# A Mamba-2 scan block's share of the carried state: per-head products against a decayed C, or one 512-column product scaled by token and added by identity products

## The chip, the core and the metric

One core of a Trainium2 chip runs the whole program. The metric is device time in microseconds: 2370.83 us is the median of three timed runs (2366.95 to 2382.75). Five engines work side by side, each through its own instructions in order: TensorE (PE, matrix products; PEld its weight loads), VectorE (DVE), ScalarE (ACT), GpSimd (POOL) and SyncE (SP, which issues DMAs). The tensor engine's clock has two levels in the records, 2.4 GHz (a granted clock of 1.00) and 1.2 GHz (0.50).

## The reference, cut to what matters

The model is two layers deep; layer 0 has a Mamba-2 mixer, layer 1 attention, both between feed-forward blocks. A prompt of 512 tokens and a running stream of 32 tokens (with its old state) go through together. The mixer has 32 heads of 64 channels in 4 groups of 8, and a state of 128 numbers for each channel. The scan that the change touches:

```python
def step(state, inp):
    x_c, a_c, B_c, C_c = inp
    a_cs = jnp.cumsum(a_c, axis=1)
    seg = a_cs[:, :, None] - a_cs[:, None, :]
    decay = jnp.exp(jnp.where(causal, seg, -jnp.inf))
    cb = jnp.einsum('bign,bjgn->bijg', C_c, B_c)
    y_diag = jnp.einsum('bijg,bijge,bjgep->bigep', cb, decay, x_c)
    y_off = jnp.einsum('bign,bgepn->bigep', C_c, state) * jnp.exp(a_cs)[..., None]
    w_end = jnp.exp(a_cs[:, -1:] - a_cs)
    new_state = state * jnp.exp(a_cs[:, -1])[..., None, None] + jnp.einsum(
        'bjgn,bjge,bjgep->bgepn', B_c, w_end, x_c)
    return new_state, y_diag + y_off
```

`y_off` is the share of the carried state in a block's outputs: C times the state, times a decay that depends on token and head alone.

## The kernel before

The kernel takes 128 tokens to a block: four blocks c = 0 to 3 of the prompt and a tail, c = 4, with the 32 tokens of the running stream. Channels lie on partitions and tokens in the free dimension, so `y` is [channels, tokens].

All dense products, written to the PSUM tile `mm`, split each float32 matrix into a high and a low part (`whi`, `wlo`) and make three products per chunk, each in two halves of 272 columns. In the Mamba layer the dense units run in the order of `MSEQ`, "i0 z0 i1 i2 z1 o0 i3 z2 o1 z3 o2 o3": inputs (B, C and four x units), gates and output products of the four groups. Each input unit goes through a short convolution (`cu`, `cv` on DVE and ACT) before the scan reads it. The buffers of B, C and x (`grp`) exist twice, so the inputs of group 2 start when the scan of group 0 is complete.

The order of all instructions is made at build time by `Plan`: every piece of work is a generator that asks for an engine ("T", "V", "W" for DVE reading PSUM, "S", "G") with an estimated cost, for a slot of a buffer ("get", "put") or for an event ("wait", "set"). `Plan.run` always takes the request that can start first, ranked by the chains' order, and what it emits is kept in that program order on each engine. Dense products have the last rank and fill what the scan leaves free. The estimated costs set the order only.

For each group g and block c the function `ssd` starts these chains: `turn_x` (four PE transposes of x, then `xd` = x times dt on DVE, `xw` on POOL), `turn_b` (transpose of B, `btok`), `decay` (the product of C and B, masked to `cb` on DVE; the decay factors `ex` by eight ACT instructions, an exponential, and DVE's product with `cb`), `state` (one 512-column product `xw,btok`, and the new state `st` by POOL and DVE), and `output`. The tile `ab` holds the running sums of a for all 8 heads, copied to all 128 partitions by a DMA from `acs_d` (`load_ab`).

The share of the carried state goes like this before: `decay_ab` (line 1176 on) exponentiates `ab` in place on ACT, copies its last column to `fade` on DVE, and for c > 0 multiplies it by C on POOL, giving eight decayed copies of C, [128, 8 x n]. `output` then adds to each head's product `ex,xd` a second product `ab,st` (the head's state as weights, its decayed C as moving data) in the same PSUM region. A head has 64 channels, so two heads fill the 128 output partitions, one in each column half of the array.

Of the kernel before, what the change touches and what calls it, by code (L numbers as in the profile page):

```python
# [4 lines left out]
F32 = mybir.dt.float32  # L5
# [5 lines left out]
P = 128  # L11
# [167 lines left out]
def _body(tc, io):  # L179
# [22 lines left out]
    with ExitStack() as ctx:  # L202
# [734 lines left out]
        def mamba(norm, after, ready, ahead):  # L937
            with tc.tile_pool(name="mt", bufs=1, reuse_waits="tile") as tmp, \
# [6 lines left out]
                def aux():  # L945
                    return pa.tile([P, 512], F32, tag="aux", name="aux")

                plan = Plan({"mm": 2, "aux": 4, "raw": 2, "w": 2, "cu": 2, "cv": 2, "grp": 2, "z": NZB, "y": NY, "yh": NYH,
                             "ab": 2, "ex": 2, "xd": 2, "xw": 2, "cb": 1, "btok": 1, "st": 3, "fade": 2}, "m")
                chunks = [(c * P, P) for c in range(NCH)] + [(TP, TS)]  # L950
                tok = tmp.tile([P, 5, 96], F32, tag="tok", name="tok")
                cstate = tmp.tile([P, 24, 6], F32, tag="cstate", name="cstate")
# [7 lines left out]
                def steps(ps):  # L960

                    cost = v_cost(T)
                    yield "wait", "r"
                    rv = halves(norm.r[:, :])
                    v = hm("dv", "ex", 2)
                    yield "W", cost, lambda: V.tensor_tensor(out=halves(v[:, :]), in0=ps[0:32, :, :H], in1=rv[0:32], op=ALU.mult)
                    yield "put", "mm"
                    yield "S", 0.15, lambda: S.activation(acoef, alog, AF.Exp), "exp"
                    yield "V", 0.08, lambda: V.tensor_scalar(acoef, acoef, -1.0, None, op0=ALU.mult)
                    yield "V", cost, lambda: V.tensor_scalar(v, v, dtb, None, op0=ALU.add)  # L970
                    e = hm("de", "ex", 2)
                    yield "V", cost, lambda: V.scalar_tensor_tensor(out=e, in0=v, scalar=-1.0, in1=v, op0=ALU.mult, op1=ALU.min)
                    yield "S", s_cost(T), lambda: S.activation(e, e, AF.Exp), "exp"
                    s = hm("ds", "xd", 2)
                    yield "V", cost, lambda: V.tensor_scalar(s, e, 2.0, None, op0=ALU.add)
                    yield "V", 3.5, lambda: V.reciprocal(s, s)
                    yield "V", cost, lambda: V.tensor_tensor(out=s, in0=s, in1=e, op=ALU.mult)
                    s2 = hm("dw", "xd", 2)
                    yield "V", cost, lambda: V.tensor_tensor(out=s2, in0=s, in1=s, op=ALU.mult)
                    q = hm("dq", "xw", 2)  # L980
                    yield "V", cost, lambda: V.tensor_scalar(q, s2, 1.0 / 17.0, None, op0=ALU.mult)
                    for k in (15, 13, 11, 9, 7, 5, 3):
                        yield "V", cost, lambda: V.scalar_tensor_tensor(out=q, in0=q, scalar=1.0 / k, in1=s2, op0=ALU.add, op1=ALU.mult)
                    yield "V", cost, lambda: V.scalar_tensor_tensor(out=q, in0=q, scalar=1.0, in1=s, op0=ALU.add, op1=ALU.mult)
                    yield "V", cost, lambda: V.tensor_scalar(q, q, 2.0, None, op0=ALU.mult)
                    dtt = hm("dt", "st", 3)
                    yield "V", cost, lambda: V.scalar_tensor_tensor(out=dtt, in0=v, scalar=0.0, in1=q, op0=ALU.max, op1=ALU.add)
                    a = hm("da", "xw", 2)
                    yield "V", cost, lambda: V.tensor_scalar(a, dtt, acoef, None, op0=ALU.mult)
                    keep = hm("keep", "ab", 2)  # L990

                    def starts():
                        G.memset(keep, 1.0)
                        for c in range(5):
                            G.memset(keep[:, c * P:c * P + 1], 0.0)
                    yield "G", 1.0, starts
                    acs = hm("acs", "st", 3)
                    yield "V", 2 * cost, lambda: V.tensor_tensor_scan(acs, keep, a, 0.0, ALU.mult, ALU.add)
                    nc.scalar.dma_start(acs_d, acs)
                    wend = hm("wend", "st", 3)  # L1000

                    def ends():
                        for o, n in chunks:
                            S.activation(wend[:, o:o + n], acs[:, o:o + n], AF.Exp, scale=-1.0, bias=acs[:, o + n - 1:o + n])
                    yield "S", 5 * s_cost(P), ends, "exp"
                    for c, (o, n) in enumerate(chunks):
                        yield "get", "aux"
                        pt = aux()

                        def turn():  # L1010
                            for j, src in enumerate((acs, dtt, wend)):
                                TE.transpose(pt[:n, j * 32:(j + 1) * 32], src[:, o:o + n], ident[:32, :32])
                        yield "T", 0.3, turn
                        yield "W", v_cost(96), lambda: V.tensor_copy(tok[:n, c, :], pt[:n, 0:96])
                        yield "put", "aux"
                    yield "set", "tok"

                def scale():
# [155 lines left out]
                    yield "set", ("ex", g, c)  # L1174

                def decay_ab(g, c, ab):
                    off, n = chunks[c]
                    src = off if c < 4 else SOFF
                    ct = got["C", g][:, src:src + n]
                    yield "S", s_cost(8 * n), lambda: S.activation(ab, ab, AF.Exp), "exp"  # L1180
                    yield "get", "fade"
                    fade = got["fade", g, c] = tmp.tile([P, 8, 1], F32, tag="fade", name="fade", bufs=2)
                    yield "V", 0.08, lambda: V.tensor_copy(fade, ab[:, :, n - 1:n])
                    yield "set", ("fade", g, c)
                    if c > 0:
                        yield "G", 0.06 + 8 * n * 2.28e-3, lambda: G.tensor_tensor(out=ab, in0=ab, in1=ct.unsqueeze(1).to_broadcast([P, 8, n]), op=ALU.mult)
                    yield "set", ("cd", g, c)

                def turn_x(g, c):
                    off, n = chunks[c]  # L1190
# [75 lines left out]
                def output(g, c):  # L1266
                    off, n = chunks[c]
                    src = off if c < 4 else SOFF
                    xs = got["x", g]
                    need = [("ex", g, c), ("xd", g, c), ("xw", g, c), ("cd", g, c)]  # L1270
                    yield "wait", *need
                    if c > 0:
                        yield "wait", ("st", g, before(c))
                    if c == 0:
                        yield "get", "y"
                        got["y", g] = tmp.tile([P, 4, T], F32, tag="y", name="y", bufs=NY)
                        yield "set", ("y0", g)
                    else:
                        yield "wait", ("y0", g)
                    yield "get", "aux"  # L1280
                    py = aux()
                    xd, ex, ab = got["xd", g, c], got["ex", g, c], got["ab", g, c]

                    def emit(t):
                        for b in range(2):
                            h = 2 * t + b
                            dst = py[64 * b:64 * b + 64, t * P:t * P + n]
                            TE.matmul(dst, xd[:n, h, :], ex[:n, h, :], start=True, stop=c == 0)
                            if c > 0:
                                TE.matmul(dst, got["st", g, before(c)][:, h, :], ab[:, h, :], start=False, stop=True)  # L1290
                    for t in range(4):
                        yield "T", (0.24 if n < P else 0.52) if c else 0.25, lambda: emit(t)
                    yield "set", ("y", g, c)
                    yield "put", "ex"
                    yield "put", "xd"
                    yield "put", "ab"
                    pyv = py[:, :].rearrange("p (t i) -> p t i", t=4)[:, :, :n]
                    yv = got["y", g][:, :, off:off + n]

                    def skip(t):  # L1300
                        V.scalar_tensor_tensor(out=yv[:, t], in0=xs[:, t, src:src + n], scalar=dskip[:, 4 * g + t:4 * g + t + 1], in1=pyv[:, t],
                                               op0=ALU.mult, op1=ALU.add)
                    for t in range(4):
                        yield "W", v_cost(n) + 0.06, lambda: skip(t)
                    yield "put", "aux"
                    yield "set", ("out", g, c)

                def ssd(g):
# [3 lines left out]
                    for c in range(5):  # L1312
                        yield "spawn", turn_x(g, c)
                        yield "spawn", turn_b(g, c)
                        yield "spawn", decay(g, c)
                        yield "spawn", state(g, c)
                        yield "spawn", output(g, c)
                        if c < 4:
                            yield "wait", ("ex", g, c)
# [776 lines left out]
```

## Time and profile before

| | before |
|---|---|
| median of three runs | 2370.83 us (2366.95 to 2382.75) |
| the profiled execution, its own time | 2376.65 us |
| its span, first to last instruction | 2374.9 us |
| PE busy | 2315.3 us, 97% |
| DVE busy | 1753.1 us, 74% |
| ACT busy | 1057.4 us, 45% |
| POOL busy | 608.1 us, 26% |
| mean granted clock of PE | 0.981 |

The Mamba layer's scan lies between about 462 and 778 us of the span. Most instructions are recorded by one helper (line 191), so rows are told apart by their tiles: `mm<-xh,whi` is a dense product, `aux<-ex,xd` an output product of the scan. A float32 product is two records in the trace; `x4` of a 64-wide form is a pair of heads. In a row of the timeline the first number is the start, the second the time to the group's last end; ends of matmuls are modelled and overlap the next one's start, so the distance from start to start is the better measure.

### The profile page before, as it was taken

Reading aid. Unit: us, or ns where it says so; the run is one execution under the profiler, and the core shown is the slowest. Engines: PE = TensorE matmul, PEld = TensorE weight load, DVE = VectorE, ACT = ScalarE, POOL = GpSimd, SP = SyncE. Lnnn points to the kernel's source line nnn. Section 1 sums busy time; section 2 is a strip of 40 time slices with the busy share of each in tenths; the row PEclk is TensorE's granted clock in tenths of the full one; section 3 lists DMA queues with packets and bytes.
Section 4 is the critical chain, followed back from the end, with each engine's and each line's share of the span. In section 5 each row is a group of like instructions: output and inputs, shape, how many; then the busy total and the mean of one; then the engine's idle time right before and its main releaser. Section 6 shows DMA issues by size and latency. Waiting matters only on the chain.

```text
span 2374.9 us, 42488 instructions
## 1 busy us (share of the span) xinstructions
PE 2315.3 (97%) x17687; PEld 2220.8 (94%) x17694; DVE 1753.1 (74%) x2268; ACT 1057.4 (45%) x1542; POOL 608.1 (26%) x582
## 2 busy tenths in 40 slices
PE   8999999989999999999999999999999999999997
PEld 8999999979999999999999899999964799999997
DVE  7777786777767677777857877777678687777757
ACT  5333334476646343333354433333578553333344
POOL 3222222244323132122211222221334132221214
PEclk9999999989999999999999999999999999999999
DMA  4233322333333232333233332332211132333232
GB/s 156 82 97 104 93 72 89 101 94 104 88 100 96 80 107 72 106 91 103 65 102 98 116 98 83 97 103 68 88 41 32 36 107 81 103 94 102 64 103 74
DMA packets 113617, 213.15 MB, mean 90 GB/s; under 512 B 12529, under 2 KB 34545, under 8 KB 113425
## 3 DMA queue, kind: packets, MB, share of 16 engines
q1 hardware_dynamic: 110640, 204.92, 28.3%
q10 hardware_dynamic: 2784, 5.52, 0.7%
q8 instruction: 139, 2.28, 0.4%
q14 instruction: 54, 0.43, 0.1%
HBM read 204.83 MB, written 5.58 MB: 89 GB/s over the span
## 4 chain that ended last, share of the span: by engine, by line
PE 90%; DVE 5%; ACT 2%; issue 1%; DMA 1%; POOL 0%; SPq 0%; DVEq 0%; ACTq 0%; POOLq 0%
PE mm L191 79%; PE z L191 5%; PE aux L191 4%; DVE wlo L191 1%; PE f L191 1%; PE o L191 1%; DVE xl L191 1%; ACT whi L191 1%; DVE x L191 1%; DVE sl L191 0%; DMA wraw<-in_wpg 0%; DVE hl L191 0%; DVE fu L191 0%; DMA wraw<-in_wgu 0%; ACT zt L191 0%
## 5 line engine op out<-in xcount | busy, mean ns | idle before, releaser
L191 PE MATMUL mm<-xh,whi 128*128 128x272 f32 x1976 | 498.2, 295 | 2.0 <-ACT xh L191 1.4
L191 PE MATMUL mm<-xl,whi 128*128 128x272 f32 x1976 | 493.0, 293 | 3.0 <-DVE xl L191 3.0
L191 PE MATMUL mm<-xh,wlo 128*128 128x272 f32 x1976 | 490.5, 291 | 3.4 <-DVE wlo L191 3.4
L191 PE MATMUL mm<-xfh,whi 128*128 128x272 f32 x1248 | 363.2, 291 | 14.2 <-ACT c L191 11.6
L191 PE MATMUL mm<-xfl,whi 128*128 128x272 f32 x1248 | 362.5, 290 | 0.0
L191 PE MATMUL mm<-xfh,wlo 128*128 128x272 f32 x1248 | 362.2, 290 | 0.0
L191 PEld LDWEIGHTS mm<-xh,whi 128*128 128x128 f32 x1976 | 345.7, 192 | 11.2 <-issue 7.8
L191 PEld LDWEIGHTS mm<-xl,whi 128*128 128x128 f32 x1976 | 345.8, 192 | 4.0 <-DVE xl L191 3.9
L191 PEld LDWEIGHTS mm<-xh,wlo 128*128 128x128 f32 x1976 | 345.3, 192 | 4.3 <-DVE wlo L191 4.3
L191 ACT ACTIVATE whi<-wraw 128x1024 fp32r<-128x1024 f32 (+3 forms) x205 | 175.4, 857 | 379.9 <-PE mm L191 257.5
L191 DVE TENSOR_TENSOR wlo<-wraw,whi 128x1024 fp32r<-128x1024 f32 (+3 forms) x247 | 249.1, 1009 | 65.5 <-ACT whi L191 55.0
L191 PE MATMUL mm<-hh,whi 128*128 128x272 f32 x1408 | 291.3, 288 | 0.0
L191 ACT ACTIVATE whi<-a 128x1024 fp32r<-128x1024 f32 x133 | 141.2, 1061 | 336.8 <-PE mm L191 212.2
L191 PE MATMUL mm<-hh,wlo 128*128 128x272 f32 x1408 | 290.9, 288 | 0.0
L191 PE MATMUL mm<-hl,whi 128*128 128x272 f32 x1408 | 290.9, 288 | 0.0
L191 DVE TENSOR_TENSOR wlo<-a,whi 128x1024 fp32r<-128x1024 f32 x154 | 191.5, 1243 | 100.4 <-ACT whi L191 63.6
L191 PEld LDWEIGHTS mm<-xfh,whi 128*128 128x128 f32 x1248 | 237.5, 190 | 15.6 <-ACT c L191 11.0
L191 PEld LDWEIGHTS mm<-xfh,wlo 128*128 128x128 f32 x1248 | 237.7, 190 | 0.0
L191 PEld LDWEIGHTS mm<-xfl,whi 128*128 128x128 f32 x1248 | 237.7, 190 | 0.0
L191 PEld LDWEIGHTS mm<-hl,whi 128*128 128x128 f32 x1408 | 221.2, 188 | 0.0
L191 PEld LDWEIGHTS mm<-hh,whi 128*128 128x128 f32 x1408 | 221.0, 188 | 0.0
L191 PEld LDWEIGHTS mm<-hh,wlo 128*128 128x128 f32 x1408 | 220.7, 188 | 0.2 <-DVE wlo L191 0.2
(290 smaller groups left out, 4290.9 us busy)
## 6 DMA issues: line engine op xcount, KB each, us to landing
a<-in_wgu SPq DMA_DIRECT2D x156, 512.0 KB, 3.9
wraw<-in_wd SPq DMA_DIRECT2D x128, 256.0 KB, 2.7
wraw<-in_win SPq DMA_DIRECT2D x41, 512.0 KB, 3.6
wraw<-in_wd SPq DMA_DIRECT2D x32, 384.0 KB, 3.2
wraw<-in_wgu SPq DMA_DIRECT2D x18, 512.0 KB, 3.7
ab<-acs_d SPq DMA_DIRECT2D x16, 512.0 KB, 4.7
wraw<-in_wout SPq DMA_DIRECT2D x16, 512.0 KB, 3.6
wraw<-in_wpg SPq DMA_DIRECT2D x16, 512.0 KB, 3.6
```

Of the source, the lines that this page charges most:

```text
L191: ins = getattr(self.engine, op)(*args, **kw)
```

## The change

`ab` is no longer exponentiated and no longer multiplied by C. `decay_ab` only makes `fade`, by a small ACT exponential of the last column, and returns the buffer. A new table `etok`, the exponential of the running sums in token-major form, is made once. A new chain `carry_on` makes, for c > 0, one product of 512 columns, C (as weights) times the state of all 8 heads, giving [tokens, 8 x 64] in a PSUM slot of `aux`; DVE scales it by `etok` on the way out into `yo`. `output` adds `yo` with four products against the identity, which also turn it to [channels, tokens]. These use the whole width of the array. The estimated costs of `output` change too, and so the order that `Plan` makes.

```diff
@@ -946,7 +946,7 @@
                     return pa.tile([P, 512], F32, tag="aux", name="aux")
 
                 plan = Plan({"mm": 2, "aux": 4, "raw": 2, "w": 2, "cu": 2, "cv": 2, "grp": 2, "z": NZB, "y": NY, "yh": NYH,
-                             "ab": 2, "ex": 2, "xd": 2, "xw": 2, "cb": 1, "btok": 1, "st": 3, "fade": 2}, "m")
+                             "ab": 2, "ex": 2, "xd": 2, "xw": 2, "cb": 1, "btok": 1, "st": 3, "fade": 2, "yo": 2}, "m")
                 chunks = [(c * P, P) for c in range(NCH)] + [(TP, TS)]
                 tok = tmp.tile([P, 5, 96], F32, tag="tok", name="tok")
                 cstate = tmp.tile([P, 24, 6], F32, tag="cstate", name="cstate")
@@ -1013,6 +1013,12 @@
                         yield "T", 0.3, turn
                         yield "W", v_cost(96), lambda: V.tensor_copy(tok[:n, c, :], pt[:n, 0:96])
                         yield "put", "aux"
+                    etok = got["etok"] = tmp.tile([P, 5, 32], F32, tag="etok", name="etok")
+
+                    def grown():
+                        S.activation(etok[:, 0:4, :], tok[:, 0:4, 0:32], AF.Exp)
+                        S.activation(etok[:TS, 4, :], tok[:TS, 4, 0:32], AF.Exp)
+                    yield "S", 0.5, grown, "exp"
                     yield "set", "tok"
 
                 def scale():
@@ -1174,17 +1180,29 @@
                     yield "set", ("ex", g, c)
 
                 def decay_ab(g, c, ab):
+                    n = chunks[c][1]
+                    yield "get", "fade"
+                    fade = got["fade", g, c] = tmp.tile([P, 8, 1], F32, tag="fade", name="fade", bufs=2)
+                    yield "S", 0.12, lambda: S.activation(fade, ab[:, :, n - 1:n], AF.Exp), "exp"
+                    yield "set", ("fade", g, c)
+                    yield "put", "ab"
+
+                def carry_on(g, c):
+
                     off, n = chunks[c]
                     src = off if c < 4 else SOFF
-                    ct = got["C", g][:, src:src + n]
-                    yield "S", s_cost(8 * n), lambda: S.activation(ab, ab, AF.Exp), "exp"
-                    yield "get", "fade"
-                    fade = got["fade", g, c] = tmp.tile([P, 8, 1], F32, tag="fade", name="fade", bufs=2)
-                    yield "V", 0.08, lambda: V.tensor_copy(fade, ab[:, :, n - 1:n])
-                    yield "set", ("fade", g, c)
-                    if c > 0:
-                        yield "G", 0.06 + 8 * n * 2.28e-3, lambda: G.tensor_tensor(out=ab, in0=ab, in1=ct.unsqueeze(1).to_broadcast([P, 8, n]), op=ALU.mult)
-                    yield "set", ("cd", g, c)
+                    yield "wait", ("st", g, before(c)), ("in", g, 5)
+                    yield "get", "yo"
+                    yield "get", "aux"
+                    po = aux()
+                    st = got["st", g, before(c)]
+                    yield "T", 0.9, lambda: TE.matmul(po[:n, :], got["C", g][:, src:src + n], st[:, :, :].rearrange("p h d -> p (h d)"), start=True, stop=True)
+                    yield "set", ("y", g, c)
+                    yo = got["yo", g, c] = tmp.tile([P, 8, 64], F32, tag="yo", name="yo", bufs=2)
+                    yield "W", v_cost(512), lambda: V.tensor_tensor(out=yo[:n], in0=po[:n, :].rearrange("p (h d) -> p h d", d=64),
+                                                                  in1=got["etok"][:n, c, 8 * g:8 * g + 8].unsqueeze(2).to_broadcast([n, 8, 64]), op=ALU.mult)
+                    yield "put", "aux"
+                    yield "set", ("yo", g, c)
 
                 def turn_x(g, c):
                     off, n = chunks[c]
@@ -1267,10 +1285,8 @@
                     off, n = chunks[c]
                     src = off if c < 4 else SOFF
                     xs = got["x", g]
-                    need = [("ex", g, c), ("xd", g, c), ("xw", g, c), ("cd", g, c)]
+                    need = [("ex", g, c), ("xd", g, c), ("xw", g, c)] + ([("yo", g, c)] if c else [])
                     yield "wait", *need
-                    if c > 0:
-                        yield "wait", ("st", g, before(c))
                     if c == 0:
                         yield "get", "y"
                         got["y", g] = tmp.tile([P, 4, T], F32, tag="y", name="y", bufs=NY)
@@ -1279,21 +1295,22 @@
                         yield "wait", ("y0", g)
                     yield "get", "aux"
                     py = aux()
-                    xd, ex, ab = got["xd", g, c], got["ex", g, c], got["ab", g, c]
+                    xd, ex = got["xd", g, c], got["ex", g, c]
 
                     def emit(t):
                         for b in range(2):
                             h = 2 * t + b
                             dst = py[64 * b:64 * b + 64, t * P:t * P + n]
-                            TE.matmul(dst, xd[:n, h, :], ex[:n, h, :], start=True, stop=c == 0)
-                            if c > 0:
-                                TE.matmul(dst, got["st", g, before(c)][:, h, :], ab[:, h, :], start=False, stop=True)
+                            TE.matmul(dst, xd[:n, h, :], ex[:n, h, :], start=True, stop=c == 0, skip_group_check=True)
+                        if c > 0:
+                            TE.matmul(py[:, t * P:t * P + n], got["yo", g, c][:n, 2 * t:2 * t + 2, :].rearrange("p h d -> p (h d)"), ident[:n, :n],
+                                      start=False, stop=True, skip_group_check=True)
                     for t in range(4):
-                        yield "T", (0.24 if n < P else 0.52) if c else 0.25, lambda: emit(t)
-                    yield "set", ("y", g, c)
+                        yield "T", (0.45 if n < P else 0.7) if c else 0.45, lambda: emit(t)
                     yield "put", "ex"
                     yield "put", "xd"
-                    yield "put", "ab"
+                    if c > 0:
+                        yield "put", "yo"
                     pyv = py[:, :].rearrange("p (t i) -> p t i", t=4)[:, :, :n]
                     yv = got["y", g][:, :, off:off + n]
 
@@ -1314,6 +1331,8 @@
                         yield "spawn", turn_b(g, c)
                         yield "spawn", decay(g, c)
                         yield "spawn", state(g, c)
+                        if c > 0:
+                            yield "spawn", carry_on(g, c)
                         yield "spawn", output(g, c)
                         if c < 4:
                             yield "wait", ("ex", g, c)
```

PE, the end of group 0's scan (`ident,xs` are the transposes of x, `xw,btok` the state product, `32x128` and `32x32` those of the tail). Before, from the last dense product on:

```order
L191 MATMUL mm<-xh_4329,wlo 128x272 x2
L191 MATMUL aux<-ident,xs 128x128 x4
L191 MATMUL aux<-ident,B 128x128
L191 MATMUL aux<-C,B 128x128
L191 MATMUL aux<-ex,xd 64x128
L191 MATMUL aux<-ab,st 64x128
```

After, from the last dense product on:

```order
L191 MATMUL mm<-xh_4329,wlo 128x272 x2
L191 MATMUL aux<-st,C 128x512
L191 MATMUL aux<-xw,btok 128x512
L191 MATMUL aux<-ex,xd 64x128 x2
L191 MATMUL aux<-ident,yo 128x128
L191 MATMUL aux<-ex,xd 64x128 x2
L191 MATMUL aux<-ident,yo 128x128
```

Before, block 3's transposes and the outputs of blocks 2, 3 and 4 stand behind the last dense product (8 pairs of rows `ex,xd` and `ab,st` for each); after, those of blocks 3 and 4, and block 4's transposes stand behind block 3's outputs. The pair `ex,xd x2` and `ident,yo` comes four times a block.

PE, the tail of group 1, before:

```order
L191 MATMUL mm<-xh_4289,wlo 128x272 x2
L191 MATMUL aux<-ex,xd 64x32
L191 MATMUL aux<-ab,st 64x32
L191 MATMUL aux<-ex,xd 64x32
L191 MATMUL aux<-ab,st 64x32
```

And after:

```order
L191 MATMUL mm<-xh_4289,wlo 128x272 x2
L191 MATMUL aux<-ex,xd 64x32 x2
L191 MATMUL aux<-ident,yo 128x32
L191 MATMUL aux<-ex,xd 64x32 x2
L191 MATMUL aux<-ident,yo 128x32
```

Sixteen alternating rows become eight; the tail's own `st,C` product stands 84 dense records earlier, next to its state product.

DVE, block 3 of group 0 after the change (`cu` is the read-out of a dense unit, `wlo` a weight's low part):

```order
L191 TENSOR_TENSOR cb<-aux,upper 128x128
L191 SCALAR_TENSOR_TENSOR y<-xs,vecs,aux 128x128
L191 TENSOR_TENSOR cu<-mm,r 128x272
L191 TENSOR_TENSOR cu<-mm,r 128x240
L191 TENSOR_TENSOR cu<-mm,r 128x32
L191 TENSOR_TENSOR wlo<-wraw,whi 128x1024
L191 TENSOR_TENSOR yo<-aux,etok 128x512
L191 SCALAR_TENSOR_TENSOR cv<-cu,vecs,cv 128x547 x3
L191 TENSOR_TENSOR ex<-ex,cb 128x1024
L191 TENSOR_TENSOR st<-st,aux 128x512
```

The scaling `yo` is new in this queue, behind `cu` and `wlo`; the copy `fade`, which came after `ex` before, is gone from it.

## Rows read from the trace of the kernel before

**Rows 1.** The page's first part: engine, busy us, share of the span, instructions.

```profile
PE 2315.3 (97%) x17687; PEld 2220.8 (94%) x17694; DVE 1753.1 (74%) x2268; ACT 1057.4 (45%) x1542; POOL 608.1 (26%) x582
```

**Rows 2.** Table by stage: stretch, its length, busy us by engine, granted clock, DMA.

```profile
core 0: us, PE busy (x) PEld busy (x) DVE busy (x) ACT busy (x) POOL busy (x), PEclk, DMA share, GB/s
540.00:830.00 290.00, 290.00 (x2323) 274.17 (x2322) 211.65 (x365) 158.29 (x259) 88.53 (x97) 0.96 0.31 95
...
500.30:530.70 30.40, 21.91 (x137) 16.01 (x136) 19.75 (x43) 18.27 (x36) 13.72 (x13) 0.72 0.29 80
```

**Rows 3.** The chain that ended last: start us, length us, what.

```profile
515.00 2.35 POOL ab L191
...
530.71 7.67 PE mm L191 x48
```

**Rows 4.** Timeline of PE, the tail of group 1: start us, us, operation.

```profile
583.11 0.30 PE L191 MATMUL aux<-ex,xd 32*64 32x32 f32 x2
583.34 0.30 PE L191 MATMUL aux<-ab,st 128*64 128x32 f32 x2
...
588.10 0.66 PE L191 MATMUL mm<-xl,whi 128*128 128x272 f32 x2
588.55 0.65 PE L191 MATMUL mm<-xh,wlo 128*128 128x272 f32 x2
```

**Rows 5.** Table by stage, the tails of groups 1 to 3 and what follows.

```profile
583.00:592.20 9.20, 9.20 (x55) 8.30 (x54) 3.84 (x9) 3.07 (x4) 0.83 (x4) 0.63 0.27 64
660.90:670.70 9.80, 9.80 (x59) 8.98 (x58) 5.83 (x14) 3.57 (x5) 1.06 (x4) 0.66 0.38 94
770.70:780.00 9.30, 9.30 (x55) 8.44 (x54) 5.88 (x11) 1.44 (x3) 0.65 (x1) 0.63 0.20 56
585.40:592.20 6.80, 6.80 (x35) 6.41 (x34) 3.42 (x8) 1.61 (x2) 0.00 (x0) 0.50 0.35 82
664.00:670.70 6.70, 6.70 (x32) 6.51 (x32) 4.77 (x12) 1.90 (x2) 1.06 (x4) 0.50 0.47 106
```

**Rows 6.** Instructions on `ab`, `fade` and `xd`: count, ns minimum, median, maximum, span, forms.

```profile
L191 ACT ACTIVATE ab<-ab x20: 399/1043/1047, 475.3 to 760.6; 128x1024 f32<-128x1024 f32 x16, 128x256 f32<-128x256 f32 x4
L191 DVE COPY fade<-ab x20: 151/165/605, 476.7 to 766.3; 128x8 f32<-128x8 f32 x20
L191 POOL TENSOR_TENSOR ab<-ab,C x16: 734/2387/2416, 492.9 to 768.0; 128x1024 f32<-128x1024 f32 x12, 128x256 f32<-128x256 f32 x4
...
L191 DVE TENSOR_TENSOR xd<-aux,tok x20: 672/684/692, 463.2 to 752.0; 128x512 f32<-128x512 f32 x16, 32x512 f32<-32x512 f32 x4
```

**Rows 7.** Timeline of PE, outputs of block 1 of group 0, dense products ahead.

```profile
496.64 0.42 PE L191 MATMUL mm<-xl,whi 128*128 128x272 f32 x2
496.90 0.41 PE L191 MATMUL mm<-xh,wlo 128*128 128x272 f32 x2
...
497.73 0.44 PE L191 MATMUL aux<-ex,xd 128*64 128x128 f32 x4
497.95 0.44 PE L191 MATMUL aux<-ab,st 128*64 128x128 f32 x4
```

**Rows 8.** The chain: outputs of c = 0, transposes, a state product, a full block's outputs.

```profile
478.65 1.95 PE aux L191 x23
...
538.38 0.77 PE aux L191 x7
...
541.41 0.86 PE aux L191 x2
...
645.67 1.95 PE aux L191 x32
```

**Rows 9.** Timeline, group 0: DVE's `cu` and `wlo`, then block 3's `C,B` and `ex`.

```profile
486.03 0.85 DVE L191 TENSOR_TENSOR cu<-mm,r 128x272 f32<-128x272 f32 x3 [1.52 <-PE mm L191]
486.92 1.23 DVE L191 TENSOR_TENSOR wlo<-wraw,whi 128x1024 fp32r<-128x1024 f32 x1
...
503.76 0.49 PE L191 MATMUL aux<-C,B 128*128 128x128 f32 x2 [1.40 <-DVE xd L191]
...
513.55 1.23 DVE L191 TENSOR_TENSOR ex<-ex,cb 128x1024 f32<-128x1024 f32 x1
```

## The prediction

> **What bounds the kernel now.** The page comes first: PE is busy for 97% of the span, the next engine, DVE, for 74% [rows 1]. That is an average, so the table by stage comes next, cut around the Mamba layer. From 540 to 830 us, where groups 1 to 3 of the scan run among the dense products, PE is busy for 290.00 of 290.00 us, and the only loss is the granted clock, 0.96 [rows 2]. From 500.3 to 530.7, the end of group 0's scan, PE is busy for only 21.91 of 30.40 us at 0.72 [rows 2]. The reader should see two regimes: in the long one a microsecond of PE work is a microsecond of the kernel and relief for ACT, POOL or DVE is worth nothing; in the short one PE waits for the scan.
>
> The chain shows why the short one exists. In this stretch POOL's product `ab` (C times decay) stands in the chain with 2.35 us from 515.00, just before PE goes on, and the first long piece of dense (`mm`) products comes at 530.71 [rows 3]. The first product of group 2 needs the buffers of group 0, so nothing dense is left until the last output of group 0 is written.
>
> The third thing to see are the tails, the sample stream's 32 tokens (c = 4). Their 16 head products of 32 columns start 0.23 us apart each [rows 4], although they stream a quarter of the columns. The dense products behind them start 0.45 us a pair, where 0.25 is usual [rows 4, 7]. The table by stage gives the reason: from 585.40 on, 2.3 us after the first narrow product, the granted clock is 0.50, the lower of the two levels (1.2 GHz), for 6.8 us, in group 2 for 6.7 us [rows 5], and the tail of group 3 has the same mean as that of group 1, 0.63 [rows 5]. What PE did before the fall was the narrow products.
>
> **The change, part by part.**
>
> *Work taken from ACT, POOL and given to DVE.* ACT loses 16 exponentials of 1.04 us and 4 of 0.40, some 18 us, and gets 20 tiny ones of 8 columns and the new `etok`. POOL loses 12 products of 2.39 us and 4 of 0.73, 31.6 us. DVE loses 20 copies of 0.17 and gains 16 scalings `yo` out of PSUM; `xd`, of the same shape and kind of operands, takes 0.68, so DVE gains 10.9 − 3.4 = 7.5 us [rows 6]. In groups 1 to 3 all of this lies under PE: DVE has 211.65 busy of 290 us there [rows 2], and three quarters of 7.5 us make it about 217. If that cover were gone, DVE's part alone would cost 5.6 us. The earlier return of the `ab` buffer lets its DMA start earlier; that too is hidden there. All this is costed at nothing outside group 0.
>
> *PE, full blocks.* Before, a block's outputs (c > 0, 128 tokens) are one stretch of 32 records; the chain gives it 1.95 us from dense product to dense product, and a plain 512-column product 0.86 [rows 8]. Within it, four records of a pair of heads start 0.22 us apart: `ex,xd` of both heads, then `ab,st` of both [rows 7]. The two heads of a pair run side by side in the two column halves. Eight steps of 0.22 are 1.76, so entering and leaving the 64-wide arrangement costs 1.95 − 1.76 = 0.19. The c = 0 block has four such steps, 0.88, and takes 1.95 together with 0.77 of transposes [rows 8]; that leaves 0.30. I take 0.25, between them.
> Now, per block: one product of 512 columns, 0.86. Then, four times: a pair of `ex,xd`, 0.22; an identity product of 128 columns on the full width, a quarter of the 512-column one, 0.215; and entering and leaving the 64-wide form, 0.25. That is 4 × 0.685 = 2.74 in place of 1.95. Per block +0.79 + 0.86 = +1.65, and for the nine full blocks of groups 1 to 3 **+14.9 us**. Bounds: if the four extra changes of form cost nothing, 4 × 0.435 + 0.19 = 1.93, so +0.84 a block, +7.6 in all. If every change costs what it seems to cost in the tail, where form changes at nearly each product, namely 0.23 less 0.05 of streaming (a quarter of 0.215), 0.18, a block takes 4 × (0.22 + 0.215 + 0.36) = 3.18: +2.09 a block, +18.8. I stay at the middle because a full block's own rows are the nearest.
>
> *PE, tails.* The excess of a tail over dense work: 9.20, 9.80 and 9.30 us with 55, 59 and 55 records [rows 5], of which 32 are the tail's; the other 23, 27 and 23 are worth 0.1255 us each at the upper level (two in 0.25 [rows 7]). That leaves 6.3, 6.4 and 6.4: 19.1 us for the three. Now a tail has 4 pairs and 4 identities: eight changes of form of 0.23 instead of sixteen products, 1.85 us, and the 512-column product, 0.86, about 2.8 with entry: 8.4. If the clock stays up, the three tails save **10.7 us**. The fall came 2.3 us into the narrow products in group 1 and 3.1 us in group 2 [rows 5]; the new stretch lasts 1.9, so I take no fall. If the clock falls all the same, 6.8 us at dense pairs of 0.45 instead of 0.25 lose 3.0 each, and the saving is 1.7.
>
> *Group 0.* Counted in the order lists, 310 dense records stand ahead of group 2's first from the `tok` transposes on, before and now, but only two outputs (c = 3, 4) behind the last of them instead of three. PE's path in the new order starts 18 records, 2.3 us, later than before, about 464.9. To the end of the last product before the dry stretch it has 228 records, 28.6 us; four rounds of transposes at 0.77, four state products and three of the new ones at 0.86; and outputs of 1.2, 2.74 and 2.74: 44.4 us, so about 509.3, with block 3's transposes done some 3.2 earlier, at 506. Before, block 3's `C,B` product started at 503.76 and the DVE product that completes `ex` ended at 514.78, 11.0 us later [rows 9]. The same 11.0 from 506 gives 517; ACT's dropped exponential (1.04) is the most that comes off, 516. PE has stood idle by then as it does before [rows 2], so output 3 runs at the lower level, where `mm` pairs take 1.8 times as long [rows 4]: 2.74 becomes 4.9, ending at 521. Block 4's transposes (before, ahead of output 3) now come behind it, then the two 512-column products, the small `ex` and the tail: 0.8 + 1.7 + 2 + 1.9, at a mixed clock some 7, then 1 us of DVE's last sums: the first dense product about 528. Before, it is 530.7 [rows 3], with one state product (0.86) of group 1 already done. **−2 us.** Bounds: −12, if block 3's factors are ready when PE comes, and +4, if the later transposes and `yo` cost another 6.
>
> **Sum:** 14.9 − 10.7 − 2 = +2.2 us. The profiled execution took 2376.65 (its span 2374.9 and 1.75 around it), which gives 2378.9; it stands 5.8 above the median of the three timed runs, 2370.83, and the forecast goes with the median: **2373 us**.
>
> **The rivals.**
> *Every change of form is dear* (chance 0.2). The tail's 0.18 holds everywhere: 18.8 − 10.7 + 0 = +8, and with clock falls in the tails, whose stretch also grows, +17: 2379 to 2388. For it: the tail rows. Against: the full block's 0.19 to 0.30 for a pair of changes, not 0.36. The Trainium skill, TensorEngine Tiling, section Key Properties, speaks on this side: changing the tiling mode, and not only the tile, drains the engine, and this change goes from two changes of form a block to eight. By that rule alone the sum would be this rival's; by the block's own rows it is the forecast's, and the trace agrees with the rule at the tails (0.23 us a product).
> *`yo` becomes the wait* (0.15, slower side). PE issues in order: an output that waits for DVE's `yo` holds the dense products behind it. In the new DVE order of group 0, `cu` (0.85) and `wlo` (1.23) stand ahead of a `yo` [rows 9]: 2.1 us. If each of the 12 blocks of groups 1 to 3 waited so long, 25 us, and the clock with it: about 2398. It decides where the lead is shorter than 2.1 + 0.68 us. Against: in the new order the shortest lead in these groups is 18 dense records and a 512-column product, 2.3 + 0.86 = 3.1 us.
> *The scan runs ahead and changes are cheap* (0.15). −12 + 7.6 − 10.7 = −15: 2356. For it: POOL's 2.3 us left the chain [rows 3]. Against: PE now does more ahead of the dry stretch, and ACT's and DVE's part of the chain stays. More than this cannot come back: idle time and clock are all that PE lost here.
> The forecast has 0.5.
>
> **How the numbers follow.** The low end is the last rival's 2356, less one for the spread of medians: 2355. The high end is the first rival with its clock falls, 2388, and 3 more for the same: 2391. About 2 in 10 is outside, most of it above. A measurement here tells about 1% (24 us) from no change. Faster by that needs more than PE lost in the layer: 0.05. Slower is most of the `yo` rival and a corner of the first: 0.16. The rest, 0.79.
>
> **What would show it.** Right: PE still without waits from 540 on; a full block's outputs near 2.7 us with a 0.86 product some 2 to 5 us ahead; tails near 1.9 us with the clock at the upper level behind them; the first dense product of group 2 around 528; POOL some 31 us less. Wrong: waits of PE for `yo`; the clock falling behind tails as before; blocks of 1.9 or over 3.1 us; a dry stretch that ends before 520 or after 534.

## The result, and the profile after

The changed kernel takes 2383.32 us (median of 20 runs, 2379.1 to 2385.47), the kernel before 2370.76 (20 runs, 2364.03 to 2382.95). The ratio is 1.0043, 95% interval 1.003 to 1.0056: slower by 0.43%. The medians are 12.6 us apart, the means of the 20 runs 9.9 (2382.99 and 2373.05), where +2.2 was forecast. The time lies inside the range given, but well off its point: in the band that the rival of dear changes of form named, 2379 to 2388.

The page's busy times of the changed kernel (engine, us, share, instructions), to be held against [rows 1]:

```profile
PE 2323.9 (98%) x17591; PEld 2211.5 (93%) x17598; DVE 1762.9 (74%) x2264; ACT 1040.0 (44%) x1541; POOL 571.2 (24%) x567
```

POOL has lost 36.9 us (31.6 forecast) and ACT 17.4 (some 18), DVE has gained 9.8 (7.5), and the time is longer all the same. PE has 96 records fewer, six in each of the 16 blocks with c > 0, and is busy for 8.6 us more. The table by stage of the changed kernel (length, busy us of PE, PEld, DVE, ACT, POOL, granted clock, DMA), beside [rows 2]:

```profile
540.00:830.00 290.00, 290.00 (x2180) 260.33 (x2175) 214.16 (x355) 144.94 (x257) 61.51 (x85) 0.99 0.32 91
...
760.00:790.00 30.00, 30.00 (x214) 25.81 (x213) 19.13 (x33) 8.66 (x17) 3.75 (x4) 0.94 0.17 53
```

PE is as full as before, at a better clock, 0.99 instead of 0.96, and yet starts only 2180 records in the stretch instead of 2323. Of these 143 fewer, 72 are by design (twelve blocks of groups 1 to 3); the rest is work that the stretch no longer held. The second row is the one place in it with a fall of the clock, behind the third tail. The chain of the changed kernel (start us, length us, what), beside [rows 3] and [rows 8]:

```profile
515.48 6.35 PE aux L191 x28
...
531.84 2.33 PE mm L191 x12
...
567.07 3.92 PE aux L191 x31
...
597.08 2.27 PE aux L191 x24
```

A full block's outputs with their 0.77 us of transposes take 3.92, so 3.15 alone, where 1.95 stood before. A tail's outputs take 2.27. Group 2's first dense product comes at 531.84, not earlier than before. The timeline of PE in the same full block of the changed kernel, beside [rows 7]:

```profile
567.00 0.44 PE L191 MATMUL aux<-ex,xd 128*64 128x128 f32 x4
567.37 0.49 PE L191 MATMUL aux<-ident,yo 128*128 128x128 f32 x2
567.79 0.44 PE L191 MATMUL aux<-ex,xd 128*64 128x128 f32 x4
568.16 0.49 PE L191 MATMUL aux<-ident,yo 128*128 128x128 f32 x2
```

From pair to pair it is 0.79 us, where the work alone is 0.22 + 0.215. The rest, 0.355, is two changes of form, nearly 0.18 each. PE's waits in the layer, from 440 to 840 us (line waited for: us, times, longest), name no `yo`:

```profile
PE aux L191 <- DVE ex L191: 5.9, 1, 5.9
PE aux L191 <- DVE xd L191: 0.3, 1, 0.3
```

### The profile page after: what moved, and what is told of

It is laid out like the page before. It is cut to its first block, busy times and chain, and to the rows that moved or that the text cites. A ratio compares the mean times of both kernels' runs of the same rounds, so it can differ in the third digit from the quotient of the medians.

```text
span 2382.0 us, 42247 instructions
## 1 busy us (share of the span) xinstructions
PE 2323.9 (98%) x17591; PEld 2211.5 (93%) x17598; DVE 1762.9 (74%) x2264; ACT 1040.0 (44%) x1541; POOL 571.2 (24%) x567
## 4 chain that ended last, share of the span: by engine, by line
PE 90%; DVE 5%; ACT 2%; issue 1%; DMA 1%; POOL 0%; SPq 0%; DVEq 0%; ACTq 0%; POOLq 0%
PE mm L191 79%; PE z L191 5%; PE aux L191 5%; DVE wlo L191 1%; PE f L191 1%; PE o L191 1%; DVE xl L191 1%; ACT whi L191 1%; DVE x L191 0%; DMA wraw<-in_wpg 0%; DVE sl L191 0%; DVE fu L191 0%; DVE hl L191 0%; DMA x<-in_x 0%; ACT zt L191 0%
```

## The experiments

Theory A: what the change costs is PE work in groups 1 to 3, above all the changes between the 64-wide and the full-width form. Rival B: the identity product's own weight load makes it long. A third, that a product waits for the one whose sum it adds to, is out for the full blocks by [rows 7]: there `ab,st` adds to the region of the `ex,xd` just ahead of it, in the same form, and starts 0.22 us behind it, with no excess. Rivals on other places: the new order; POOL's product and group 0's end; the clock behind the tails. Ratios stand against runs of the kernel before on the same chip.

### e1: the changed kernel, outputs grouped

```diff
-def emit(t):
-    for b in range(2):
...
-    if c > 0:
-        TE.matmul(py[:, t * P:t * P + n], got["yo", g, c]..., ident[:n, :n], start=False, stop=True, ...)
-for t in range(4):
-    yield "T", (0.45 if n < P else 0.7) if c else 0.45, lambda: emit(t)
+def emit():
+    for t in range(4):
+        for b in range(2):
...
+    for t in range(4 if c > 0 else 0):
+        TE.matmul(py[:, t * P:t * P + n], got["yo", g, c]..., ident[:n, :n], start=False, stop=True, ...)
+yield "T", 4 * ((0.45 if n < P else 0.7) if c else 0.45), emit
```

In e1, and in e2 below, every `ex,xd` product still carries its start flag; grouped like this, a part of the sums is lost. The instructions, their order and their sizes are those of f2 (for e1) and f1 (for e2), which set the flag once for each column half and keep the sums whole.

> The changed kernel with one thing moved: in each block's outputs the eight 64-wide products ex,xd come first and the four full-width identity products behind them, so the array changes form twice a block instead of eight times; every other engine's order is the same. Theory A (each change of form costs PE some 0.18 us): a full block's outputs fall from 3.15 us to 4 x 0.22 + 4 x 0.215 + 0.36 = 2.1, a tail's from 2.27 to about 1.0; nine blocks and three tails under a full PE give 9.5 + 3.8 = 13 us, so about 2370 us, within 0.2% of before. Theory B (the identity product's own weight load, two records of 0.19 us, is what makes it 0.42 instead of 0.215): a block stays at 2.8 to 3.1 us and the time at 2380 us or more.

Measured: 2365.23 us (12 runs, 2362.31 to 2366.53), ratio 0.9969 (0.9956 to 0.9982). The chain of e1: 36 dense records of group 2 (behind its first 12 and a state product; the changed kernel reaches them at 535.03), a full block's outputs with transposes, a tail:

```profile
525.21 4.52 PE mm L191 x36
...
556.34 2.88 PE aux L191 x31
...
584.95 1.59 PE aux L191 x24
```

2.88 − 0.77 = 2.11 us a block: theory A's figure. The identity products and their weight loads are all still there, so rival B falls for the full blocks. Six changes fewer are worth 3.15 − 2.11 = 1.04 us, 0.173 each. The tail came to 1.59, not 1.0; f2 below shows what is left in it. Grouping gave 18 us, more than the 13 expected: nine blocks and three tails give 9.4 + 2.0, and the end of group 0, which the theory had left out, came 9.8 us earlier (525.21 against 535.03); 1.1 of these stood there before the scan began (first outputs at 475.49 against 476.58 us).

### e2: the kernel before, tails grouped

Only the tail's products (n < P) are moved; `dst` is head h's place in the bank as before.

```diff
+def tail():
+    for h in range(8):
+        TE.matmul(dst, xd[:n, h, :], ex[:n, h, :], start=True, stop=False, ...)
+    for h in range(8):
+        TE.matmul(dst, got["st", g, before(c)][:, h, :], ab[:, h, :], start=False, stop=True, ...)
-    yield "T", (0.24 if n < P else 0.52) if c else 0.25, lambda: emit(t)
+    yield "T", (0.24 if n < P else 0.52) if c else 0.25, lambda: emit(t) if n == P else tail() if t == 3 else None
```

> The kernel before with one thing moved: in the tails (c = 4) the eight ex,xd products come first and the eight ab,st products behind them, instead of alternating; nothing else differs. Theory A: the alternation of 32-row and 128-row forms is what makes a tail's outputs 3.65 us long and lets the granted clock fall; grouped they take about 1.3 us, the clock behind them stays at 1.00, and each tail of groups 1 to 3 gives back up to 4.7 us, 14 us where an execution had all three falls: 2357 to 2364 us. With it, if the falls are what spreads the runs of before over 2364 to 2383 us, these runs lie within 8 us. Rival (narrow products cost 0.23 us whatever stands beside them): 3.65 us and the falls stay, no change.

Measured: 2355.66 us (6 runs, 2349.56 to 2358.75), ratio 0.9928 (0.9905 to 0.9951). The same 32 records of a tail take 1.17 us in the chain; alternating they took 4.0 to 4.4 in the first profile, the start of the fall included. The rival is out. The time lies just under the 2357 to 2364 expected. The runs span 9.2 us, where 8 was expected, against 17.5 for the 26 of the kernel before that ran with them; six runs against 26 say little on a spread. In a tail grouping also moves each `ab,st` away from the `ex,xd` that it adds to, so of the 32-column products the runs don't tell the change of form from a wait for that sum.

### e3: the kernel before without POOL's product

```diff
-yield "G", ..., lambda: G.tensor_tensor(out=ab, in0=ab, in1=ct..., op=ALU.mult)
+yield "G", ..., lambda: None
```

> The kernel before without POOL's product of the decay with C (the carried state's share is then computed without C); the order of all other instructions is the same. If POOL's product holds the end of group 0's scan, as two waits of PE for it say (1.50 and 1.16 us), the first long dense piece of group 2 comes 2 to 5 us earlier than 530.7 and the time falls by as much, to 2366 to 2369 us; groups 1 to 3 don't move. Rival (the chain of ex on ACT and DVE paces the scan, POOL's product lies beside it): under 1 us.

Measured: 2366.52 us (10 runs, 2361.68 to 2370.82), ratio 0.9977 (0.9959 to 0.9995). The chain of e3:

```profile
517.11 7.12 PE aux L191 x34
524.23 6.39 PE mm L191 x48
```

Group 2 starts 6.5 us earlier than in [rows 3]. Of these, 2.4 us stood there at the scan's first outputs (476.17 against 478.59): this execution had no fall of the clock in its first 100 us. From those outputs to group 2 it takes 48.1 us, the five profiles of the kernel before (f4 and on) take 50.3 to 54.8. So POOL's product did hold the end of group 0, and its removal is worth some 2 to 7 us there, about 5.6 in the medians (1.2 to 9.7 by the interval). The changed kernel has removed it too and starts group 2 at 531.84: the gain was there and was spent on the way.

### e4: the changed kernel with the old cost estimates

```diff
-yield "T", (0.45 if n < P else 0.7) if c else 0.45, lambda: emit(t)
+yield "T", (0.24 if n < P else 0.52) if c else 0.25, lambda: emit(t)
```

> The changed kernel with the planner's cost estimates of the output products as they were before (0.52, 0.24, 0.25 instead of 0.7, 0.45, 0.45), so with the same instructions in another order. Theory A (the loss is work on PE in groups 1 to 3): the same time within 3 us, 2380 to 2386. Rival (the new order costs it, by what it does at the end of group 0's scan): 2371 to 2376 us with the first dense product of group 2 before 528.

Measured: 2384.16 us (7 runs, 2381.84 to 2388.25), ratio 1.0051 (1.0033 to 1.0069). The first dense product of group 2 comes at 531.17, and a full block's outputs with transposes take 3.92 again. The order is not the cause.

### f1: the kernel before, tails grouped, one start flag

The edit of e2, and in it:

```diff
-TE.matmul(dst, xd[:n, h, :], ex[:n, h, :], start=True, stop=False)
+TE.matmul(dst, xd[:n, h, :], ex[:n, h, :], start=t == 0, stop=False)
```

> The kernel before with the tail's products grouped as in e2, and the start flag only on the first product of each column half of the bank, so that every later product adds or fills; same instructions and order as e2. Expected: as e2, 2355.7 us within 3, tails of 1.17 us, no clock fall behind them.

Measured: 2355.26 us (6 runs, 2352.9 to 2359.33), ratio 0.9927 (0.9903 to 0.995): faster than both kernels. Its chain at the tail of group 1, and its table by stage around the three tails:

```profile
576.72 1.17 PE aux L191 x32
```

```profile
core 0: us, PE busy (x) PEld busy (x) DVE busy (x) ACT busy (x) POOL busy (x), PEclk, DMA share, GB/s
570.00:600.00 30.00, 30.00 (x253) 28.39 (x249) 25.63 (x48) 16.52 (x27) 10.16 (x14) 1.00 0.41 115
640.00:670.00 30.00, 30.00 (x271) 28.69 (x270) 24.51 (x46) 14.96 (x25) 7.81 (x18) 1.00 0.40 124
745.00:775.00 30.00, 30.00 (x262) 29.77 (x261) 20.09 (x30) 11.01 (x14) 7.20 (x6) 1.00 0.23 80
```

No fall of the clock is left behind the tails.

### f2: the changed kernel, outputs grouped, one start flag

The edit of e1, and in it:

```diff
-TE.matmul(dst, xd[:n, h, :], ex[:n, h, :], start=True, stop=c == 0, skip_group_check=True)
+TE.matmul(dst, xd[:n, h, :], ex[:n, h, :], start=t == 0, stop=c == 0, skip_group_check=True)
```

> The changed kernel with its outputs grouped as in e1 and the start flag as in f1; same instructions and order as e1. Expected: as e1, 2365 us within 3. Against f1 it carries, in nine full blocks, the 512-column product (0.86) and 0.16 more per output stretch (2.11 against 1.95), 9.2 us, and in three tails 0.86 + 0.42: 3.8 us; less what group 0 gives, 2 to 4 us: 9 to 11 us slower than f1.

Measured: 2365.68 us (12 runs, 2364.84 to 2368.36), ratio 0.9975 (0.9962 to 0.9989): faster than the kernel before, and 10.4 us behind f1, as worked out. The timeline of PE in a full block of f2:

```profile
556.88 1.09 PE L191 MATMUL aux<-ex,xd 128*64 128x128 f32 x16
557.90 1.16 PE L191 MATMUL aux<-ident,yo 128*128 128x128 f32 x8
558.89 0.60 PE L191 MATMUL aux<-ident,xs 128*128 128x128 f32 x4
```

Sixteen records in 1.02 us, eight in 0.99, one change between them. And in the tail of group 1:

```profile
585.52 0.65 PE L191 MATMUL aux<-ex,xd 32*64 32x32 f32 x16
586.10 1.07 PE L191 MATMUL aux<-ident,yo 32*128 32x32 f32 x8
587.11 0.52 PE L191 MATMUL mm<-xh,whi 128*128 128x272 f32 x2
```

Eight identity records of 32 columns take 1.01 us, as long as eight of 128 columns; the columns don't set their time here, and a tail's rest over the expected 1.0 us is theirs. Their eight weight loads take 0.96 us in the same trace, so for the tails rival B may hold. The chain at the start of group 2:

```profile
521.99 2.55 PE mm L191 x12
...
525.93 4.53 PE mm L191 x36
```

The changed kernel has the same two pieces at 531.84 and 535.03. Of the 9.1 us at the second, 1.3 stood there at the scan's first outputs (475.27 against 476.58). So grouping is worth 7.8 us in group 0, where the granted clock from 500 to 540 us is 0.87 instead of 0.74, and 11.9 us more up to the last group's sums (789.29 against 810.31), near the 9 × 1.04 + 3 × 0.68 = 11.4 that the blocks and tails give. With both kernels grouped, the old form of the carried share is the cheaper one for a full PE: what f2 gains on the kernel before is the grouping and not the new share.

### f3: f1 with group 0 in the changed form

Groups below `NEW` get the changed `decay_ab`, `carry_on` and the grouped outputs of f2, the others stay as in f1.

```diff
+NEW = 1
...
-need = [("ex", g, c), ("xd", g, c), ("xw", g, c), ("cd", g, c)]
+need = [("ex", g, c), ("xd", g, c), ("xw", g, c)] + ([("cd", g, c)] if g >= NEW else [("yo", g, c)] if c else [])
```

> f1 with group 0 alone in the changed form (512-column product, yo, identity products, grouped as in f2), groups 1 to 3 in the form before. If POOL's product and ACT's exponential of ab hold group 0's end (e3: 6 us), and the new form's added PE work lies in PE's waits there, the first dense product of group 2 comes near 525 instead of 527 and the time is 2350 to 2354 us. Rival (the new PE work of 4 blocks, some 4 us, is paid ahead of the dry stretch): 2355 to 2359 us, as f1 or worse.

Measured: 2357.79 us (7 runs, 2356.63 to 2362.2), ratio 0.994 (0.9918 to 0.9963). The chain of f3:

```profile
513.44 4.85 PE aux L193 x28
...
525.68 1.36 PE mm L193 x6
```

Group 2 starts at 525.68, as early as hoped, but the time is no better than f1's: the rival. f1's own first long dense piece comes at 525.88 with the state product done that f3 still has before it; f3 has 42 records of group 2 left at 528.94, f1 about 2.3 us earlier. So nothing was left to gain there.

### f4, g1, g2 and g3: the kernel before, profiled again

No edit. The first profile showed three full falls behind the tails; these four ask whether every execution does.

> The kernel before once more, unchanged, for another profiled execution. If the clock's fall behind the tails comes and goes from execution to execution, this one shows another number of falls than the three of the first profile, and its time follows by up to some 3 us a fall; with three falls again it is near 2376 us, with fewer near 2365 to 2372. Rival (the falls are the same in every execution): three falls, whatever the time.

Measured: 2375.83 us, three falls of 6.8 us again. That left the rival standing, so three more:

> The kernel before, unchanged, for another profiled execution; both so far took 2376 us and had three full falls of the clock (6.8 us each) behind the tails of groups 1 to 3. If the falls explain why the median execution is 5 us faster, an execution near or under 2370 us shows fewer or shorter falls there or at the end of group 0's scan, about 3 us of time for 6.8 us of fall. Rival: three full falls at any time, and the spread comes from elsewhere.

> The kernel before, unchanged, one more profiled execution, for the same question: near or under 2370 us with fewer or shorter falls of the clock behind the tails or at the end of group 0's scan; or, by the rival, three full falls whatever the time.

> The kernel before, unchanged, a third profiled execution for the same question: time and falls go together, some 3 us for 6.8 us at the lower level; or, by the rival, three full falls whatever the time.

Measured: 2366.78, 2369.77 and 2376.68 us. Their tables by stage from 540 to 830, and around the three tails (columns as above), in this order, g1, g2, g3:

```profile
540.00:830.00 290.00, 290.00 (x2360) 274.95 (x2360) 213.38 (x365) 160.15 (x260) 88.24 (x95) 0.98 0.33 97
570.00:600.00 30.00, 30.00 (x238) 27.93 (x237) 21.80 (x41) 15.02 (x25) 9.53 (x16) 0.94 0.37 106
650.00:680.00 30.00, 30.00 (x233) 28.23 (x229) 22.58 (x42) 13.14 (x23) 6.68 (x16) 0.94 0.40 115
760.00:790.00 30.00, 30.00 (x230) 29.20 (x230) 17.75 (x27) 11.01 (x14) 6.03 (x5) 0.94 0.25 80
```

```profile
540.00:830.00 290.00, 290.00 (x2357) 274.43 (x2356) 214.51 (x371) 160.01 (x261) 89.51 (x100) 0.98 0.33 96
570.00:600.00 30.00, 30.00 (x236) 27.61 (x235) 21.78 (x47) 15.20 (x25) 11.38 (x16) 0.94 0.36 103
650.00:680.00 30.00, 30.00 (x227) 28.01 (x228) 19.86 (x40) 11.86 (x21) 7.44 (x15) 0.89 0.36 107
760.00:790.00 30.00, 30.00 (x241) 29.20 (x242) 18.17 (x28) 10.21 (x15) 7.21 (x6) 1.00 0.31 85
```

```profile
540.00:830.00 290.00, 290.00 (x2324) 274.17 (x2323) 210.57 (x366) 157.23 (x257) 88.11 (x99) 0.96 0.32 94
570.00:600.00 30.00, 30.00 (x232) 27.07 (x229) 20.15 (x44) 15.82 (x25) 11.63 (x18) 0.89 0.40 110
650.00:680.00 30.00, 30.00 (x225) 27.01 (x221) 19.95 (x41) 10.77 (x20) 8.38 (x11) 0.89 0.34 98
760.00:790.00 30.00, 30.00 (x211) 28.12 (x211) 17.74 (x29) 10.31 (x21) 5.35 (x5) 0.89 0.25 69
```

A mean of 0.89 over 30 us is a fall of some 6.6 us (0.11 × 30 at half the clock), 0.94 about half of that, 1.00 none. The execution of 2366.78 us has three half falls, the one of 2369.77 one half, one full and none, those of 2376 us three full ones. Time and falls go together; the same program has falls of another length in another execution. The forecast's own profile was one of the dear ones. Not all of the 10 us between them lies in the tails: the end of group 0 differs too. The stretch from 500 to 540 and the chain's first long dense piece of group 2, in g1 and in g3:

```profile
500.00:540.00 40.00, 31.40 (x214) 25.19 (x213) 28.17 (x59) 26.33 (x52) 17.32 (x19) 0.83 0.25 70
529.21 6.90 PE mm L191 x48
```

```profile
500.00:540.00 40.00, 30.80 (x178) 24.21 (x177) 24.66 (x50) 24.76 (x48) 13.75 (x13) 0.70 0.26 70
533.47 7.69 PE mm L191 x48
```

The other three start group 2 at 530.71, 532.75 (f4) and 533.18 (g2). The last group's sums (`acc,ones`) come at 793.75 in g1 and at 802.92 in g3: of the 9.9 us between the two executions 9.2 are made by then, 4.3 of these by the start of group 2.

## Why the prediction was right or wrong

**What bounds the kernel: right.** PE stays full from 540 to 830, and neither what POOL lost there nor what ACT lost there counts. No wait for `yo` appears, so that rival is out, and the lead of 3.1 us or more was enough.

**Full blocks: the mechanism right, the size wrong.** This is the first step that failed, by a sign that the forecast itself had named (a block over 3.1 us): "I take 0.25, between them" for entering and leaving the 64-wide form. It measured 0.355, and a block 3.15 instead of 2.74, so 3.15 − 1.95 + 0.86 = +2.06 a block and +18.5 in place of +14.9. That is the upper bound, taken from the tail's rows. I held a block that enters and leaves the form once to be the nearest row. Its 0.19 was a remainder, 1.95 less eight steps read as 0.22 each, and two hundredths in a step are 0.16 in it; why one pair of changes beside dense products measures less than the pairs inside a block is not settled. The tail's alternating rows showed the change of form itself, and were the better witness. The rival "every change of form is dear", given 0.2, was the true case for this term. The Trainium skill, TensorEngine Tiling (Array Packing), section Key Properties, says that changing the mode drains the engine; the trace agrees, at 0.173 us a change (e1), and the forecast should have followed it.

**Tails: right, with a remainder.** They went from 6.3 us of excess each to 2.27 + 0.86 = 3.13, forecast 2.8. The clock held behind the first two; behind the third it fell for some 3.4 us. That makes −9.7 plus about 1.5, near −8.2 for the profiled execution, where −10.7 was forecast. What was mis-sized is "eight changes of form of 0.23", 1.85 us: f2 shows that the identity products of 32 columns are long by themselves.

**Group 0: the gain did not come.** Forecast: the first dense product at 528, −2 us. Measured: 531.84, against 530.71 before with 0.86 us of group 1's work already done, so +2.0 against this one execution. The five profiles of before start group 2 anywhere from 529.21 to 533.47, so the sign is not settled; a gain of 2 us does not show. Block 3's factors came as reckoned (PE goes on at 515.48; 516 was said). What was mis-sized is the rest at the lower level of the clock: output 3 took 5.3 us instead of 4.9, the two 512-column products 3.8 instead of 1.7 us, the tail 3.7 instead of 1.9. The working had set them "at a mixed clock"; the clock stayed at 0.50 from 515.5 to 533. e3 shows that the gain on POOL's product was real, about 5.6 us; f2, with the same products grouped, starts group 2 at 521.99, and 1.3 us of that lead come from ahead of the scan.

**The sum on the profiled executions.** 18.5 − 8.2 + 2.0 = +12.3 worked out; at the last group's sums (`acc,ones`), the same place in both programs, the changed kernel is 10.2 us behind (810.31 against 800.14); 2 us between the two figures are not accounted for. Behind that point it gets 3 us back, where the execution of before had falls of the clock that this one has not (0.96 from 1780 to 2000 us, against 0.98); the profiled executions differ by 7.1 in all (2383.72 and 2376.65).

**The second step that failed: from one execution to the median.** "It stands 5.8 above the median … and the forecast goes with the median" moved the same difference over to 2370.83. But the saving of 10.7 us in the tails was read from an execution with three full falls, and executions of 2367 and 2370 us have half of them (g1, g2). The kernel before is the one with falls to lose; the changed one keeps within 6.4 us over 20 runs and its profiled execution stands at its median. So 5.5 us of the 12.6 between the medians (2.9 of the 9.9 between the means) are no added work: the typical execution of before never had that much to give back. The clock of each run on record bears this out. Of 45 runs of the kernel before, the three at a mean clock of 0.988 took 2365.9 us on average and the four at 0.981 took 2380.1; over all 45, time and clock have a correlation of −0.91. The 0.007 between them are some 33 us more at the lower level, and 14.2 us lost in 33 is 0.43 for each us there, about what a tail's fall costs (3.0 in 6.8). So the falls make up most of the spread; what else is in it stays open.

## What to carry to other kernels

On a full PE, count how often the array's form changes, and order products of one accumulation by form before anything else is rewritten: grouping alone gave 0.7% (f1), where the rewritten share without it cost 0.4%. A price that a stretch shows only as a remainder is a weak witness; take it from rows where the same event comes many times. When the runs of a kernel spread by more than the change is worth, a saving on the clock read from one profile is not the saving of the median.

## What the runs showed of the hardware

Products that change form cost more than their columns say. In a full block each change between the 64-wide and the full-width form is worth 0.173 us (e1). Narrow products of 32 columns take 0.23 us each when 32-row and 128-row forms alternate [rows 4], and 1.17 us for all sixteen when grouped (f1).

The granted clock falls to 0.50 while PE shows no idle time at all (6.80 of 6.80 us busy [rows 5]), behind those alternating products, and how long it stays there differs between executions of one program: behind the tail of group 1 the mean over 30 us is 0.94 in g1 and 0.89 in g3. Behind the grouped products of f1 it is 1.00. The Trainium skill, TensorE: Matmul & The Clock Gate, Part 1, says that the clock's monitor runs on freely and isn't reset when a kernel starts, so that the same kernel has more or fewer slow products at its start from run to run; the page says it of the start, and here the falls in the middle differ as well.
